# A reordered layer step, an earlier root chain, and six instead of five weight tiles in freed memory, in a two-layer hybrid backbone

## The chip, the cores and the metric

One core of a Trainium2 chip runs the whole program. The metric is the device time of one execution in microseconds, as the median of a few runs. The engines are TensorE (PE, matmuls, with PEld for its weight loads), VectorE (DVE), ScalarE (ACT), GpSimd (POOL) and SyncE (SP, which here only issues DMA). A second source of DMA is POOL, for gathers and scatters through an index.

## What is computed

Two layers over 512 latent tokens and 256 context tokens, 1024 wide. Each layer is a mixer and a mixture of experts (MoE):

```python
h  = rmsnorm(x) * modulation                      # latents and context apart
p  = h @ w_in                                     # split: q, k, v | z, xbc, dt
attn = diff_attend(rope(q), rope(k), v)           # 4 heads, each with its own rms norm
ssd  = gated_group_rmsnorm(mamba2_both_ways(conv(xbc), dt), z)
x += gate * (concat(attn, ssd) @ w_out)           # layer 1: the latents alone
h2 = rmsnorm(x) * modulation
aff = softmax(h2 @ w_router)                      # 16 experts
gate, idx = top_k(aff, 2 * n / 16)                # each expert takes 64 latent, 32 context rows
x[idx] += gate * ((silu(xe @ w_gate) * (xe @ w_up)) @ w_down)   # 1024 -> 1408 -> 1024
```

## The kernel before

All matmuls of the mixer are made of three in a short float format: an operand is split into a high part (`H`, `hi`, rounded by ACT) and a low part (`L`, `lo`, the rest, a subtraction on DVE or POOL), and `mm3` adds high x high, high x low and low x high. `Pieces` streams the mixer's weights: `fetch` issues the load of a piece (`raw`), `pull` rounds it on ACT (`rt<-raw`, L131), and the subtraction follows (L143), on POOL and DVE by turns.

The order of the work on each engine is the order in which the program issues it, moved by a scheduler with priorities (`tc.high_priority()`), and by hand in stretches under `manual_schedule`. Much of the program is generators: `q.tick(f, n)` takes n steps of a main stream `f` of matmuls and lets one step of each queued side job (`q.add(...)`) go between. A DMA that waits holds up every DMA behind it on SP. Pools of tiles (`pre`, `hp`, `op`, `rb`, `gx`) lie in one memory; a pool opened where another was released takes its addresses, and its first users wait for the last users of what lay there.

**The step between the layers.** Layer 0's MoE ends with the last expert's context rows: `yc` on PE (L1565), then the tail, `add_last` (L1688 on): a scaling on ACT, a multiplication by the gate vector on POOL (`rt<-rt`, L1692), and a scatter with addition into the context rows `xc` in DRAM (L1693). Layer 1 begins with `late_norm` (L837): four loads of latent rows (`xin`), their squares summed on ACT (L855) and DVE (L853, with a scratch tile `junk`), a chain of eleven tiny DVE instructions for the inverse root (`rsqrt_steps`, L204 to L223), the scaling of the rows (ACT L864, DVE L866), transposes (`trx`), then `H`, `h` and `L`, and the first projection (`xacc`). Two context tiles (`xin<-xc`) follow in the same way, once the scatter has landed.

**The heads' end.** Four heads (`hd[0]` to `hd[3]`) are projected and attended one after the other; `attend` stores its rows (`ob`) in DRAM (`mixd`). Then the output projection runs tile by tile: `op_in` loads a tile of 128 rows (`mixin<-mixd`), computes the roots of its group norms by the same chain (tags `mrs`), scales it on ACT (L1204), transposes it on PE (`mtr`, L1210) and splits it into `mT`; `op_tile` multiplies (`oacc`). `op_setup` beside it prepares the router: `wrA`, and `rbp` (L1172), sums over its columns for the latents and for the context.

**The MoE's weights.** Per expert there are eight pairs of gate and up tiles (`gw`, 1.44 MB a pair) and eleven w_down tiles (`rt`, `wd`, 0.52 MB each). The pairs rotate through nine buffers: `ngw` in pool `rb`, the rest in `gx`, one more elsewhere. `rb` takes the memory of the heads, which comes free while the output projection runs; `gx` that of the output weights, free only at its end. `cut` says in which ticks the pairs of expert 0 are asked for.

## Time and profile before

| | |
|---|---|
| median of 3 runs | 2394.22 us (2391.91 to 2396.35) |
| the profiled execution | 2389.74 us, span 2388.0 us |
| mean granted PE clock in it | 0.970 |
| busy share of the span | PE 91%, DVE 39%, ACT 27%, POOL 18% |
| bytes moved | 701.69 MB, 294 GB/s over the span |
| mixer of layer 0, MoE of layer 0 | 0 to 545 us, 545 to 1276 us |
| mixer of layer 1, MoE of layer 1 | 1276 to 1720 us, 1720 to 2388 us |

PE's 91% is a mean over stages of different kinds. In the MoE stages the share of the DMA engines tells whether the stream of weights sets the pace; in the mixers the waits of PE are read one by one, with the engine that ended each.

### The profile page before, as it was taken

The numbers are of one execution on the slowest core, as the hardware profiler recorded it, in microseconds if no ns is written. First come the engines' busy times: TensorE is split into PE (matmuls) and PEld (weight loads), VectorE is DVE, ScalarE is ACT, GpSimd is POOL, SyncE is SP. The second block draws the span as 40 slices with busy tenths as digits, with TensorE's granted clock in tenths as the row PEclk, the third lists the DMA queues.
The fourth block names the chain that finished last, engine by engine and source line by source line (L and its number), as shares of the span: only waits on it lengthen the run. The fifth ranks groups of instructions, "written<-read, shape, count | busy, mean of one in ns | idle before, by whom it ended". The sixth has DMA issues, their size and how long they took to land. (4 is left out here: it accounts for less than half of the span.)

```text
span 2388.0 us, 49731 instructions
## 1 busy us (share of the span) xinstructions
PE 2176.3 (91%) x20620; PEld 1247.0 (52%) x20620; DVE 931.7 (39%) x2586; ACT 652.2 (27%) x1791; POOL 433.5 (18%) x554
## 2 busy tenths in 40 slices
PE   6898998999999999999987988989799999988776
PEld 4677788685444444444435667877543333232322
DVE  5787578772111111111116786786611110101010
ACT  4434477532111111111113334575101010101000
POOL 4464342000101001001003464341000000000000
PEclk9999999999999999999998999999899999999999
DMA  7323723589999999999994226334999999999997
GB/s 250 91 78 102 266 72 107 186 285 344 390 407 401 398 405 393 401 400 400 395 390 127 86 66 198 112 109 139 347 400 416 385 416 410 416 411 415 412 413 314
DMA packets 229790, 701.69 MB, mean 294 GB/s; under 512 B 30340, under 2 KB 79324, under 8 KB 229564
## 3 DMA queue, kind: packets, MB, share of 16 engines
q1 hardware_dynamic: 220076, 681.37, 73.9%
q0 software_dynamic: 9488, 17.14, 3.5%
q8 instruction: 163, 2.67, 0.4%
q14 instruction: 63, 0.52, 0.1%
HBM read 674.66 MB, written 23.76 MB: 292 GB/s over the span
## 5 line engine op out<-in xcount | busy, mean ns | idle before, releaser
L1518 PE MATMUL gl<-gw,xeT 128*32 128x512 f32 (+1 forms) x8192 | 654.8, 466 | 61.9 <-DMA gw<-w_up 59.1
L1518 PEld LDWEIGHTS gl<-gw,xeT 128*32 128x32 f32 x8192 | 279.1, 111 | 441.4 <-issue 396.5
L1559 DVE SCALAR_TENSOR_TENSOR th<-th,gl 128x256 f32<-128x256 f32 (+1 forms) x96 | 37.5, 391 | 698.5 <-ACT th L1558 698.4
L1572 PE MATMUL yl<-rt,hl 128*32 128x512 f32 x2040 | 257.7, 595 | 9.5 <-PE gl L1518 9.2
L1558 ACT ACTIVATE th<-gl 128x256 f32<-128x256 f32 (+1 forms) x96 | 35.1, 366 | 768.1 <-PE gl L1518 761.4
L179 PE MATMUL pacc<-rt,H 128*128 128x384 f32 (+1 forms) x768 | 203.1, 346 | 7.1 <-POOL rt L143 2.4
L1699 DVE SCALAR_TENSOR_TENSOR ys<-yl,gate,G2l 128x512 f32<-128x512 f32 x32 | 24.0, 751 | 380.5 <-PE yl L1572 367.4
L1609 PE MATMUL gc<-gw,xeT 128*32 128x352 f32 x2048 | 171.2, 459 | 0.0
L1700 POOL DMA_INDIRECT out<-ys,sidx x16 | 24.8, 1549 | 730.6 <-DVE ys L1699 589.8
L179 PEld LDWEIGHTS pacc<-rt,H 128*128 128x128 f32 x768 | 134.1, 192 | 19.8 <-issue 6.0
L1572 PEld LDWEIGHTS yl<-rt,hl 128*32 128x32 f32 x2040 | 70.4, 109 | 141.3 <-issue 83.2
L179 PE MATMUL xacc<-H,rt 128*128 128x512 f32 (+1 forms) x448 | 135.9, 381 | 7.0 <-ACT H L816 6.6
L1456 POOL DMA_INDIRECT xe<-xn2d,gidx x16 | 15.1, 943 | 617.6 <-PE xet L1466 507.0
L179 PE MATMUL pacc<-rt,L 128*128 128x384 f32 (+1 forms) x384 | 127.1, 331 | 0.0
L1471 ACT ACTIVATE xeT<-xet,MC,A 128x64 f32<-128x64 f32 (+1 forms) x256 | 74.1, 426 | 178.5 <-PE xet L1466 178.5
L143 POOL TENSOR_TENSOR rt<-raw,rt 128x384 fp32r<-128x384 f32 (+1 forms) x88 | 101.5, 1176 | 80.7 <-ACT rt L131 66.4
L179 PE MATMUL oacc<-woh,mT 128*128 128x512 f32 x304 | 107.4, 411 | 0.0
L1572 PE MATMUL yl<-wd,hl 128*32 128x512 f32 x776 | 102.2, 599 | 2.2 <-DMA wd<-w_down 1.7
L1609 PEld LDWEIGHTS gc<-gw,xeT 128*32 128x32 f32 x2048 | 68.8, 110 | 56.6 <-issue 44.8
L179 PEld LDWEIGHTS xacc<-H,rt 128*128 128x128 f32 x448 | 83.1, 199 | 22.9 <-ACT H L816 7.4
L179 PE MATMUL xacc<-L,rt 128*128 128x512 f32 (+1 forms) x224 | 82.6, 371 | 3.0 <-POOL L L879 2.1
L1485 PE MATMUL xpk<-x,one 128*64 128x512 f32 x256 | 81.8, 633 | 3.4 <-DVE one L1481 3.4
(410 smaller groups left out, 3279.0 us busy)
## 6 DMA issues: line engine op xcount, KB each, us to landing
gw<-w_gate SPq DMA_DIRECT2D x256, 704.0 KB
gw<-w_up SPq DMA_DIRECT2D x256, 704.0 KB
rt<-w_down SPq DMA_DIRECT2D x255, 512.0 KB
wd<-w_down SPq DMA_DIRECT2D x97, 512.0 KB
mr<-w_mod SPq DMA_DIRECT2D x80, 512.0 KB
raw<-w_in SPq DMA_DIRECT2D x48, 256.0 KB
raw<-w_in SPq DMA_DIRECT2D x64, 192.0 KB
RB<-acsd SPq DMA_DIRECT2D x20, 512.0 KB
```

Of the source, the lines that this page charges most:

```text
L143: e.tensor_tensor(lo.bitcast(F32R), x, hi, op=OP.subtract)
L179: self.nc.tensor.matmul(o, a[x].bitcast(F32R), b[y].bitcast(F32R), start=start and i == 0, stop=stop and i == 2, **kw)
L1456: self.nc.gpsimd.indirect_dma_start(out=xe[0:n], out_offset=None, in_=self.xn2d[0:rows], in_offset=bass.IndirectOffsetOnAxis(ap=idx[0:n, e ...
L1471: nc.scalar.activation(xT[:, kk, c:d], tr[:, k, c - a:d - a], AF.Identity, scale=self.A2[:, s, kk:kk + 1], bias=self.MC[:, l, s, 24 + kk:2 ...
L1485: nc.tensor.matmul(ps[64 * j:64 * j + 64], one[:, t], self.x1[t][:, 512 * j:512 * j + 512], start=t == 0, stop=t == NL - 1, skip_group_che ...
L1518: self.nc.tensor.matmul(gl[c][32 * j:32 * j + 32, o:o + n].rearrange("p (u t i) -> p u t i", u=2, i=32), self.xT[:, k, 32 * g:32 * g + 32] ...
L1558: nc.scalar.activation(th, g, AF.Tanh, scale=0.5)
L1559: nc.vector.scalar_tensor_tensor(th, th, 1.0, g, op0=OP.add, op1=OP.mult)
L1572: nc.tensor.matmul(y[64 * j + 32 * g:64 * j + 32 * g + 32], h[:, g, b], wd[b][:, 512 * j:512 * j + 512], start=b == 0, stop=b == NF - 1, s ...
L1609: nc.tensor.matmul(gc[u][32 * j:32 * j + 32].rearrange("p (t i) -> p t i", i=32), xT[:, k, 64:96], w, start=k == 0, stop=k == KD - 1, skip ...
L1699: nc.vector.scalar_tensor_tensor(ys, y, self.gate[:, i, e:e + 1], G2[i], op0=OP.mult, op1=OP.mult)
L1700: nc.gpsimd.indirect_dma_start(out=dst[i], out_offset=bass.IndirectOffsetOnAxis(ap=self.sidx[:, i, e:e + 1], axis=0), in_=ys, in_offset=No ...
```

## The change

Three places are edited. At the **layer step** the two scratch tiles of the squares are allocated ahead of the x tiles; the last expert's tail runs inside `late_norm`, between the squares and the root chain, as one DVE instruction instead of one on ACT and one on POOL; the chain is issued in one piece ahead of the first weight subtractions; and the low parts of the first two weight pieces (`quiet`) are made on DVE. At the **heads' end** the roots of the first tile are computed by `mix_roots` in the last head's last tick (tags `mrt`), the store of `ob` is issued a step earlier, `op_setup` begins two steps earlier and leaves the context's half of `wrA` and `rbp` out in layer 1, where no context row is projected, and the first output tile takes its matmuls a little earlier. In the **MoE's weights** six pairs instead of five go to the heads' memory, and two instead of three to `gx`.

```diff
@@ Pieces.__init__ / pull
-        self.net, self.todo, self.raw, self.turn, self.low = net, iter(loads), [], 0, None
+        self.net, self.todo, self.raw, self.turn, self.low, self.quiet = net, iter(loads), [], 0, None, 0
...
-        pool = self.turn % 2 or x.shape[-1] == 384 if scale is None else scale is False
+        pool = (self.turn % 2 or x.shape[-1] == 384 if scale is None else scale is False) and self.turn > self.quiet
@@ run, start of layer 1
                 with tc.high_priority():
                     next(ln)
+                W.quiet = 2
                 ws = [xbc_weights(0)]
-                self.tail()
                 next(ln)
@@ run, heads
+        self.roots = {}
...
+                    if h == 3 and tk == 11:
+                        q.add(self.first_of(self.mix_roots(l, 0)))
                     q.tick(f, 4)
...
-        cut = [range(0, 2), range(2, 4), range(4, 5)] if l == 0 else [range(0, 5)]
+        cut = [range(0, 2), range(2, 4), range(4, 6)] if l == 0 else [range(0, 6)]
...
                 if i == 0:
-                    n = (2, 1)[j > 5] if j > 1 else 0
+                    n = (2, 1)[j > 3] if j > 0 else 0
@@ late_norm
+        junks = [pre.tile([P, D], BF16, name=f"junk{i}") for i in range(2)]
         xs = [pre.tile([P, D], F32, tag="xin", name="xin", bufs=NT) for _ in range(NT)]
...
-                junk = pre.tile([P, D], BF16, tag=f"junk{t % 2}", name="junk")
+                junk = junks[t % 2]
...
             if a == 0:
+                self.tail()
+            with self.tc.high_priority():
+                rs = self.rsqrt(pre, ss[:, a:a + n], n, 1.0 / D, f"rs{a}")
+            if a == 0:
                 yield
                 load(range(NL, NT))
             with self.tc.high_priority():
-                rs = self.rsqrt(pre, ss[:, a:a + n], n, 1.0 / D, f"rs{a}")
@@ op_setup
         yield
-        yield
-        yield
...
-        for s in range(2):
+        for s in range(1 if l else 2):
@@ new, and op_in
+    def mix_roots(self, l, t):
+        n = 6 if t >= NL else 5
+        self.roots[t] = yield from self.rsqrt_steps(self.lp, self.mss[:, t, 0:n], n, 1.0, "mrt")
...
-        rs = yield from self.rsqrt_steps(op, self.mss[:, t, 0:n + 2], n + 2, 1.0, f"mrs{n}")
-        yield
+        if t in self.roots:
+            rs = self.roots[t]
+        else:
+            rs = yield from self.rsqrt_steps(op, self.mss[:, t, 0:n + 2], n + 2, 1.0, f"mrs{n}")
+            yield
@@ add_last
-        nc.scalar.activation(ys, y, AF.Copy, scale=self.gate[:, 1, e:e + 1])
-        nc.gpsimd.tensor_tensor(ys, ys, g2, op=OP.mult)
+        nc.vector.scalar_tensor_tensor(ys, y, self.gate[:, 1, e:e + 1], g2, op0=OP.mult, op1=OP.mult)
...
-    ngw = 5
+    ngw = 6
@@ Head.attend, after ob and its square
+        if not own:
+            n.st(n.mixd[self.l][t * P:(t + 1) * P, P * self.h:P * self.h + P], ob)
         yield
...
-            return
-        n.st(n.mixd[self.l][t * P:(t + 1) * P, P * self.h:P * self.h + P], ob)
```

What the scheduler makes of it at the places that matter here. First the layer step on SP, the difference with each row's waits; `xin` are the latent rows, `raw` the first weight pieces. The names of the waits are counters: DMAHW and DMASW of DMA queues, the others of engines.

```order
 L162 DMA xin<-xr 128x1024 [waits DMASW4_49,DMASW5_49,DMASW3_49,DMASW6_49,DMASW2_49,DMASW7_49,DMASW1_49,DMAHW1_49,DMASW0_49,PE_49]
-L162 DMA xin<-xr 128x1024 [waits DMAHW2_49]
+L162 DMA xin<-xr 128x1024 [waits DMAHW2_49,DMAHW0_49,PE_49]
 L162 DMA xin<-xr 128x1024 [waits DMAHW3_49]
 L162 DMA xin<-xr 128x1024 [waits DMAHW4_49]
 L162 DMA raw<-w_in 128x4x128 [waits DMAHW5_49,DVE_49]
-L162 DMA raw<-w_in 128x4x128 [waits DMAHW6_49,PE_49,Activation_49]
+L162 DMA raw<-w_in 128x4x128 [waits DMAHW6_49,Activation_49]
 L162 DMA raw<-w_in 128x4x128 [waits DMAHW7_49]
```

The loads stand in the same order, but the second `xin` waits now for PE as well. The same place on DVE, before (from the squares L853 to the scaling L866, the chain's middle left out):

```order
L853 SCALAR_TENSOR_TENSOR junk,ss<-xin 128x1024 x2
L143 TENSOR_TENSOR rt<-raw,rt 128x512
L204 TENSOR_SCALAR rs_m<-ss 128x4
L206 TENSOR_SCALAR rs_y<-rs_m 128x4
...
L217 SCALAR_TENSOR_TENSOR rs_y<-rs_q,rs_y 128x4
L143 TENSOR_TENSOR rt<-raw,rt 128x512
L219 TENSOR_TENSOR rs_e<-rs_y 128x4
L221 TENSOR_TENSOR rs_e<-rs_e,rs_h 128x4
L223 SCALAR_TENSOR_TENSOR rs_y<-rs_e,rs_y 128x4
L866 TENSOR_SCALAR xin<-xin,rs_y 128x512 x4
```

and of the change (squares L857, scaling L873; L1704 is the tail):

```order
L857 SCALAR_TENSOR_TENSOR junk_12712,ss<-xin 128x1024 x2
L1704 SCALAR_TENSOR_TENSOR rt<-yc,gate_5699,rt 128x256
L204 TENSOR_SCALAR rs_m<-ss 128x4
L206 TENSOR_SCALAR rs_y<-rs_m 128x4
...
L219 TENSOR_TENSOR rs_e<-rs_y 128x4
L221 TENSOR_TENSOR rs_e<-rs_e,rs_h 128x4
L223 SCALAR_TENSOR_TENSOR rs_y<-rs_e,rs_y 128x4
L143 TENSOR_TENSOR rt<-raw,rt 128x512 x2
L873 TENSOR_SCALAR xin<-xin,rs_y 128x512 x4
```

The two weight subtractions (L143) have moved out of and ahead of the chain to behind it, and the tail stands ahead of the chain. Then DVE at the end of layer 1's heads, before; `KK` and `QL` are the last head's operands, `nm` the maximum that its exponentials need, `mrs` and `qrs` two root chains:

```order
L1808 TENSOR_TENSOR KK<-qtr,KK 64x256 x2
L1810 TENSOR_TENSOR QL<-qtr,Q 64x256 x2
L1832 TENSOR_REDUCE nm<-sc 128x2
L1759 TENSOR_REDUCE qss<-sq 128x4
L1833 SCALAR_TENSOR_TENSOR nm<-nm,rq 128x2
L204 TENSOR_SCALAR mrs_m<-mss 128x5
L204 TENSOR_SCALAR qrs_m<-qss 128x8
L145 SCALAR_TENSOR_TENSOR rt<-raw,wmix,woh 128x512
```

and of the change, where `mrt` is the first tile's root chain:

```order
L213 TENSOR_TENSOR mrt_e<-mrt_e,mrt_m 128x5
L215 SCALAR_TENSOR_TENSOR mrt_q<-mrt_e 128x5
L217 SCALAR_TENSOR_TENSOR mrt_y<-mrt_q,mrt_y 128x5
L219 TENSOR_TENSOR mrt_e<-mrt_y 128x5
L1820 TENSOR_TENSOR KK<-qtr,KK 64x256
L221 TENSOR_TENSOR mrt_e<-mrt_e,mrt_h 128x5
L1820 TENSOR_TENSOR KK<-qtr,KK 64x256
L223 SCALAR_TENSOR_TENSOR mrt_y<-mrt_e,mrt_y 128x5
L1822 TENSOR_TENSOR QL<-qtr,Q 64x256 x2
L1844 TENSOR_REDUCE nm<-sc 128x2
L1771 TENSOR_REDUCE qss<-sq 128x4
L1845 SCALAR_TENSOR_TENSOR nm<-nm,rq 128x2
```

The chain for the first tile stood behind the maximum and its products and shared DVE with `qrs`; it ends now ahead of `QL`. Last, SP at the entry of layer 0's MoE, before, `G2l` and `G2c` being gate vectors:

```order
L162 DMA gw<-w_up 128x1408
L162 DMA rt<-w_down 128x1024
L162 DMA xr<-ctx 128x1024
L169 DMA xc<-x_5933 128x1024
L162 DMA rt<-w_down 128x1024 x3
L162 DMA gw<-w_gate 128x1408
L162 DMA gw<-w_up 128x1408
L169 DMA xn2d<-xn 128x1024
L162 DMA gw<-w_gate 128x1408
...
L162 DMA G2c<-modd 32x256 x4
L162 DMA rt<-w_down 128x1024 x2
L162 DMA wd<-w_down 128x1024 x3
```

and of the change:

```order
L162 DMA gw<-w_gate 128x1408
L162 DMA xr<-ctx 128x1024
L162 DMA gw<-w_up 128x1408
L169 DMA xc<-x_5933 128x1024
L162 DMA rt<-w_down 128x1024
L162 DMA gw<-w_gate 128x1408
L162 DMA gw<-w_up 128x1408
L169 DMA xn2d<-xn 128x1024
L162 DMA gw<-w_gate 128x1408
...
L162 DMA G2c<-modd 32x256 x4
L162 DMA rt<-w_down 128x1024 x5
L162 DMA wd<-w_down 128x1024 x3
```

The sixth pair stands ahead of the first w_down tile (`rt`), and three more w_down tiles stand behind `G2c`.

## Rows read from the trace of the kernel before

**Rows 1.** The page: DMA engines' busy tenths in 40 equal slices.
```profile
DMA  7323723589999999999994226334999999999997
```

**Rows 2.** Windows: PE, PEld, DVE, ACT, POOL busy; clock, DMA share, GB/s.
```profile
540.00:544.00 4.00, 2.69 (x15) 2.58 (x16) 1.67 (x10) 0.31 (x2) 0.77 (x1) 0.50 0.27 80
1720.00:1724.00 4.00, 3.42 (x10) 1.38 (x12) 1.19 (x5) 0.00 (x0) 0.00 (x0) 0.50 1.02 413
1728.00:1732.00 4.00, 3.92 (x46) 2.10 (x50) 1.52 (x7) 2.50 (x9) 0.00 (x0) 1.00 0.15 59
```

**Rows 3.** PE's timeline, step: start, us, instruction, idle before and releaser.
```profile
1274.00 1.94 PE L1565 MATMUL yc<-wd,hc 128*32 128x256 f32 x32
1287.40 2.82 PE L872 MATMUL trx<-ident,xin 128*128 128x128 f32 x12 [11.47 <-ACT xin L864]
```

**Rows 4.** Timeline of PE at the heads' ends of both layers.
```profile
408.03 1.33 PE L1210 MATMUL mtr<-ident,mixin 128*128 128x128 f32 x5 [2.19 <-ACT mixin L1204]
...
1608.65 1.75 PE L1210 MATMUL mtr<-ident,mixin 128*128 128x128 f32 x7 [7.99 <-ACT mixin L1204]
...
1616.12 3.64 PE L1172 MATMUL rbp<-wr,MC 128*128 128x16 f32 x32
```

**Rows 5.** Timeline of SP's queue at the step.
```profile
1265.76 2.58 SPq L162 DMA_DIRECT2D xin<-xr  x4
1268.45 3.74 SPq L162 DMA_DIRECT2D raw<-w_in  x4
...
1285.21 0.80 SPq L162 DMA_DIRECT2D xin<-xc  x2
```

**Rows 6.** Timeline of ACT at the step, the latents' squares.
```profile
1270.10 1.06 ACT L855 ACTIVATE junk<-xin 128x1024 bf16<-128x1024 f32 x1 [1.02 <-DMA xin<-xr]
...
1273.20 1.06 ACT L855 ACTIVATE junk<-xin 128x1024 bf16<-128x1024 f32 x1 [1.95 <-DMA xin<-xr]
```

**Rows 7.** Timeline of DVE at the step, squares, chain and scaling.
```profile
1275.99 1.23 DVE L853 SCALAR_TENSOR_TENSOR junk<-xin 128x1024 bf16<-128x1024 f32 x1 [4.80 <-PE yc L1565]
...
1277.26 2.17 DVE L853 SCALAR_TENSOR_TENSOR junk<-xin 128x1024 bf16<-128x1024 f32 x1
...
1280.75 3.82 DVE L207 TENSOR_SCALAR rs_h<-rs_m 128x4 f32<-128x4 f32 x1
1284.48 0.16 DVE L209 TENSOR_SCALAR rs_y<-rs_y 128x4 int32<-128x4 int32 x1
...
1285.43 0.69 DVE L143 TENSOR_TENSOR rt<-raw,rt 128x512 fp32r<-128x512 f32 x1
...
1286.43 0.16 DVE L223 SCALAR_TENSOR_TENSOR rs_y<-rs_e,rs_y 128x4 f32<-128x4 f32 x1
1286.62 1.67 DVE L866 TENSOR_SCALAR xin<-xin,rs_y 128x512 f32<-128x512 f32 x4
```

**Rows 8.** Timeline of POOL at the step, scatter and weight subtracts.
```profile
1280.28 1.74 POOL L1693 DMA_INDIRECT xc<-rt,sidx  x1 [0.28 <-POOL rt L1692]
1281.46 3.06 POOL L143 TENSOR_TENSOR rt<-raw,rt 128x512 fp32r<-128x512 f32 x2
```

**Rows 9.** Groups of PE, 1286 to 1316 us: busy, mean ns | idle, releaser.
```profile
L179 PE MATMUL xacc<-L,rt 128*128 128x512 f32 (+1 forms) x32 | 11.6, 375 | 2.1 <-POOL L L879 2.1
```

**Rows 10.** Timeline of ACT at layer 1's heads' end and a later mixin.
```profile
1600.65 0.38 ACT L1864 ACTIVATE ob<-po,rr 128x128 f32<-128x128 f32 x1
...
1604.21 0.98 ACT L1837 ACTIVATE e<-sc,nm,rq 128x768 f32<-128x768 f32 x1
...
1608.09 1.79 ACT L1204 ACTIVATE mixin<-mixin,mrs_y 128x256 f32<-128x256 f32 x5 [2.55 <-DVE mrs_y L223]
...
1668.16 0.91 ACT L1204 ACTIVATE mixin<-mixin,mrs_y 128x256 f32<-128x256 f32 x2 [1.50 <-DMA mixin<-mixd]
```

**Rows 11.** Timeline of SP's queue, mixin loads of layer 1.
```profile
1598.54 0.90 SPq L162 DMA_DIRECT2D mixin<-mixd  x2
...
1665.51 0.80 SPq L162 DMA_DIRECT2D mixin<-mixd  x2
```

## The prediction

> **What bounds the kernel now.** I read the slices of the page first. The DMA line [rows 1] stands at 9 from the 10th to the 21st slice and again from the 29th to the last but one: those are the two MoE stages, in which 256 pairs of gate and up tiles stream in. The windows say how full that is: 1720 to 1724 us moves 413 GB/s at a share of 1.02 [rows 2]. Once such a stream runs without a gap, the end of its stage is the start of the stream plus bytes over rate. So an edit pays only if it lets the stream start earlier, or takes a gap out ahead of it. Gaps do stand there: 540 to 544 us has a share of 0.27 (2.9 us unused) and 1728 to 1732 us one of 0.15 (3.4 us unused) [rows 2]. In the second, all eight tiles are loaded and the next loads wait until the first expert's matmuls release one. The mixer sets that moment, so what the mixer saves ahead of it arrives at the end nearly whole.
>
> Next I looked where the mixers stand still. At the step between the layers TensorE (PE) ends the last expert's context rows (yc) at 1274.00 + 1.94 = 1275.94 and is idle for 11.47 us, until ScalarE (ACT) has scaled the first x tile [rows 3]. At the heads' end PE is idle 7.99 us in layer 1 and 2.19 us in layer 0 [rows 4], both times for the scaling of the mixin tile on ACT.
>
> **The step between layers.** The four x tiles are asked for from 1265.76, the first four weight pieces from 1268.45 [rows 5]. The first square starts at 1270.10 (4.34 us after the load's issue), the third tile's at 1273.20: one tile each 1.55 us [rows 6]. VectorE (DVE) begins its two squares at 1275.99 because its scratch tile lies where a w_down tile of the yc matmuls was, and ends them at 1277.26 + 2.17 = 1279.4. Then comes the root chain. Its steps take 0.16 us each at some 0.2 us spacing, but one lasts 3.82 us, from 1280.75 to 1284.57, while GpSimd (POOL) runs a scatter and two weight subtracts (1280.28 to 1284.52) [rows 7, 8]. The first scaling by the roots starts at 1286.62.
>
> The change takes the 0.69 us subtract out of the chain's middle [rows 7], and the last expert's tail off ACT and POOL. Had it done only this, the chain could end at about 1279.4 + 0.5 + 11 x 0.19 = 1282.0, and with two subtracts (0.65 each) ahead of the scaling, that would begin at 1283.3, 3.3 us earlier. But the scratch tiles now come first in the memory, so the x tiles lie further up, and the order of SP shows the price: the second x load now waits for PE as well. I take that for the last yc matmul, since the tile under it is the last w_down tile. So the second, third and fourth x load and the four weight pieces queued behind them leave SP not right after the first, at about 1266.5, but at 1276.0. Counted on with 4.34 and 1.55 us they are there at 1280.3, 1281.9 and 1283.4, and the last square (1.23 us alone) ends at 1284.6, 5.2 us later than now. The tail's one DVE instruction has no row: 128x256 lies between a step of 0.16 us and a square of 128x1024 at 1.23 [rows 7]; I take 0.45. Then the chain, 2.1, and the two subtracts, 1.3: scaling from 1288.5, **1.9 us later** than now, if POOL leaves the chain alone.
>
> It need not: the scatter (1.74 us) now starts when the chain does, and a weight subtract of POOL (1.53) follows [rows 8]. Bounds: nothing, or both, 3.3 us, as one step now loses 3.66. I take the middle, 1.6: scaling 3.5 us later. The Trainium skill (SBUF — State Buffer, "Who interferes with whom") says that a DVE instruction with two SBUF inputs, or in a two-port mode, and a GpSimd instruction that reads SBUF exclude each other, the later one waiting for the other's end. The step of 3.82 us agrees with it; by that rule the whole 3.3 us would be lost, and it is a reason to keep that bound. Nothing in the rows of the chain shows whether a scatter alone does this.
>
> PE gets part back. From 1287.40 it is busy but for 2.1 us in which it waits for the low halves (L) from POOL [rows 9], and DVE now makes all latent rows first, with the context's square (1.23) and chain (2.1) moved behind them. So 0 to 2.1 us returns; I take 1.0. The context itself starts some 2 us later, behind latent matmuls that have also moved: no cost. The xc loads (1285.21 now [rows 5]) wait for the scatter and move by over 4 us, covered by the same latent matmuls. Sum of the step: **+2.5 us** (1.9 - 2.1, so about 0, to 1.9 + 3.3 = 5.2).
>
> **The heads' tails.** The first tile's roots are now computed among the last head's work, so the scaling no longer waits for the chain (1608.09 in layer 1), but for ACT's turn. ACT has the exponentials until 1604.21 + 0.98 = 1605.2 [rows 10]. They come later now, since eleven DVE instructions (at most 11 x 0.19 = 2.1 us, at least nothing where DVE waited) stand ahead of the maximum that they need; I take 1.3. Scaling from 1606.5: 1.6 us gained in layer 1 (0 to 2.9). The mixin load must be there. It stood at 1598.54; now SP has the store of ob ahead of it, and ob is written at 1600.65 + 0.38. So it leaves at about 1601.5 and, with the 2.65 us that a later pair took (1665.51 to 1668.16), lands at 1604.2 [rows 10, 11]: 1.0 us before even the present end of the exponentials, which covers it. Layer 1 also drops half of the rbp matmuls, half of 3.64 us at 1616.12 [rows 4]; other PE work is at hand behind them, so I count 1.15 (0 to 1.8). Together **-2.75** (0 to -4.7). In layer 0 the same move can win at most the 2.19 us before mtr: **-1.5** (0 to -2.2). The refilled schedule of the first output tile costs no instruction; the cover is that the same matmuls run anyway, and at worst it gives nothing.
>
> **Six tiles in the heads' memory.** No byte is added. Of the weight tiles of expert 0 the sixth is loaded before most w_down tiles. In layer 0 three of them move behind G2, 3 x 0.524 MB at 413 GB/s = 3.8 us of stream; ahead of G2 the sixth tile (1.44 MB) fills their place. If SP still keeps the queue filled, 0; if the DMA runs dry between 544 and 554 us, +3.8; the 2.9 us at 540 us [rows 2] could at best be filled. I take **0**, since SP issues as fast as loads land there. In layer 1 two w_down tiles (2.5 us) move, and the 3.4 us unused at 1728 hide that: 0.
>
> **Sum:** 2.5 - 2.75 - 1.5 + 0 = -1.75 us on the profiled 2389.74, 2388.0. The median of the three runs is 4.5 us above that execution; on it the forecast is 2392.5, called **2392**: less than the 0.2% (4.8 us) that a measurement of this kernel can tell from no change.
>
> **Rivals.**
> (a) *The tails give all that they can* and the chain runs clear of POOL: step +1, tails -4.7 and -2.2, so -5.9: 2388. For it: PE is truly idle in both places. Against: ACT is busy until just before. Chance 0.22.
> (b) *The second x load does not bind*, because the matmul that it waits for is an earlier one. Then scaling starts 3.3 us earlier, as above, and PE gets the same 1.0 back behind it: -4.3, and with the tails -8.55: 2386. Against: the wait is in the order's row, and the matmul that I name is the last use of the tile under it. Chance 0.12.
> (c) *The chain sticks behind POOL*, the other side: all three squares late (1284.6), the tail 0.45, the scatter holds the chain for 1.74, one step again loses 3.66 to POOL's subtracts, then 2.1 and 1.3: scaling at 1293.8, 7.2 us late. The context's chain, behind the latent rows now, meets POOL's L subtracts in the same way and adds up to 3.3: +10.5 - 4.25 = +6.2: 2400. It decides if the first scaling comes after 1292.4 (5.8 late, which with 3.3 is past the tails' 4.25 plus 4.8). Against: SP's late loads also make POOL's subtracts late, so they may fall behind the chain. Chance 0.20.
> (d) *Nothing of it is seen*: the six tiles only reorder the stream, the tails' gain and the step's loss cancel. That is the forecast's own case, 0.46.
>
> **The numbers.** The forecast is 2392 (0.46). (a) and (b) make 0.34 faster, (c) 0.20 slower, 0.46 within. Its own range, from the bounds that partly cancel, is 2387 to 2397; with (a) and (b) at all their bounds together (-4.3 - 4.7 - 2.2 = -11.2: 2383, and the median of few runs adds 2 to 3 us either way) and (c) up to its time, 2380 to 2400: outside it is half of (c) and little of (b).
>
> **What the profile after would show.** The second x load issued at 1276, not 1266; the last square of the latents ending near 1284.6, scaling at 1288.5 to 1292, and PE idle for 13 to 16 us instead of 11.5. At the heads' end, the wait of 7.99 us split, mtr starting near 1607 in layer 1 and 406.5 in layer 0. No new DMA gap of over 1 us between 544 and 572. The forecast is wrong if x loads leave at 1266 (then b), if PE waits after the latent rows (c), or if the mixin tile lands after the exponentials, which would take the tails' gain away.

## The result and the profile after

The changed kernel takes 2406.71 us (median of 7 runs, 2401.37 to 2409.99), the kernel before 2391.96 (7 runs on the same chip): ratio 1.0064, interval 1.0054 to 1.0074, some 15 us slower. The forecast was 2392 within 2380 to 2400. It was wrong, and the time lies past the rival on the slow side (2400). The profiled execution has a span of 2407.5 us, 19.5 over that of before, so it is a long one of its seven; its parts are read below against two profiles of before. Against the first of these the 19.5 us lie at four places: 6.6 up to the first release of a weight tile in layer 0's MoE (574.89 before, 581.52 now), 4.6 at the step between the layers, 3.7 in the heads of layer 1, where nine profiles with these heads as before differ by 3.4 among themselves, and 5.8 at the heads' end. The rest of layer 0's MoE took 1.5 less, and behind the first router matmul of layer 1 it is 0.3.

The page's DMA line (for [rows 1]), and behind it the windows at layer 0's MoE entry (columns as in [rows 2]):

```profile
DMA  7223722679999999999994226333899999999997
```

The windows:

```profile
540.00:544.00 4.00, 2.19 (x20) 2.08 (x20) 2.87 (x13) 0.96 (x3) 0.97 (x1) 0.96 0.78 262
544.00:548.00 4.00, 0.53 (x5) 0.53 (x6) 2.64 (x16) 0.31 (x2) 0.00 (x0) 0.50 1.02 330
...
576.00:580.00 4.00, 4.00 (x61) 2.54 (x57) 0.72 (x2) 0.69 (x2) 0.00 (x0) 1.00 0.48 140
580.00:584.00 4.00, 4.00 (x63) 1.92 (x59) 2.48 (x9) 0.41 (x2) 0.00 (x0) 1.00 0.36 107
```

The gap of [rows 2], in which the first gather runs, is filled, as the change has it: share 1.02 from 544 to 548. But PE is busy for only 0.53 of these four us (2.69 in the gap before), and a new gap of 4.6 us has opened at 576 to 584. What was put into the first gap came out of the second; e4, with the six tiles alone, has its second gap at 572 to 580 (shares 0.64 and 0.32).

The step between the layers, PE's timeline (for [rows 3]; `dtr`, the first transposes of the time steps, is a landmark 36 us further on):

```profile
1279.10 1.94 PE L1578 MATMUL yc<-wd,hc 128*32 128x256 f32 x32
1293.39 0.69 PE L879 MATMUL trx<-ident,xin 128*128 128x128 f32 x2 [12.35 <-ACT xin L871]
...
1333.24 0.44 PE L918 MATMUL dtr<-ident,dtq 128*128 128x128 f32 x2
```

SP's queue at the same place (for [rows 5 to 8], as the next three):

```profile
1270.96 11.40 SPq L162 DMA_DIRECT2D xin<-xr  x4
1282.46 2.35 SPq L162 DMA_DIRECT2D raw<-w_in  x4
```

ACT there, the scaling:

```profile
1292.61 2.56 ACT L871 ACTIVATE xin<-xin,rs_y 128x512 f32<-128x512 f32 x4 [2.14 <-DVE rs_y L223]
```

DVE there, the last square, the tail, the chain's first step and its long one:

```profile
1287.58 1.23 DVE L857 SCALAR_TENSOR_TENSOR junk<-xin 128x1024 bf16<-128x1024 f32 x1 [1.68 <-DMA xin<-xr]
...
1288.73 0.48 DVE L1704 SCALAR_TENSOR_TENSOR rt<-yc,gate,rt 128x256 f32<-128x256 f32 x1
1289.12 0.16 DVE L204 TENSOR_SCALAR rs_m<-ss 128x4 f32<-128x4 f32 x1
...
1290.71 1.67 DVE L221 TENSOR_TENSOR rs_e<-rs_e,rs_h 128x4 f32<-128x4 f32 x1
```

POOL there:

```profile
1289.49 1.57 POOL L1705 DMA_INDIRECT xc<-rt,sidx  x1 [20.81 <-DVE rs_y L206]
1290.56 1.79 POOL L143 TENSOR_TENSOR rt<-raw,rt 128x512 fp32r<-128x512 f32 x1
```

The four x loads take 11.40 us to leave, and the weight pieces leave behind them at 1282.46, after the end of yc (1281.04), where before they had gone 7.5 us ahead of it. The last square ends 7.8 us after yc, the chain keeps its 0.2 us spacing beside the scatter, and loses 1.5 us in one step beside POOL's subtraction. ACT scales at once behind the chain.

Layer 1's heads' end, first PE's timeline (for [rows 4]; the views of ACT, SP and DVE further on are for [rows 10, 11]):

```profile
1612.66 1.50 PE L1872 MATMUL po<-V,wT 128*128 128x128 f32 x12
...
1622.13 1.76 PE L1223 MATMUL mtr<-ident,mixin 128*128 128x128 f32 x7 [7.97 <-ACT mixin L1217]
1623.68 1.06 PE L1867 MATMUL wtr<-ident,e 128*128 128x128 f32 x4
...
1626.82 3.43 PE L1177 MATMUL rbp<-wr,MC 128*128 128x16 f32 x16
...
1632.79 2.76 PE L1872 MATMUL po<-V,wT 128*128 128x128 f32 x12
```

The same matmuls before, beside `mtr` in [rows 4]; `wtr` transposes the attention's weights, which `po` then multiplies:

```profile
1598.14 1.50 PE L1860 MATMUL po<-V,wT 128*128 128x128 f32 x12
1599.47 0.60 PE L1855 MATMUL wtr<-ident,e 128*128 128x128 f32 x4
...
1610.20 2.77 PE L1860 MATMUL po<-V,wT 128*128 128x128 f32 x12
```

Windows behind `mtr`, two of the changed kernel and one of before (columns as in [rows 2]):

```profile
1622.13:1626.13 4.00, 2.84 (x12) 2.16 (x13) 3.93 (x22) 2.91 (x7) 0.76 (x2) 0.50 0.88 294
1630.13:1634.13 4.00, 4.00 (x15) 3.52 (x16) 1.85 (x7) 0.00 (x0) 0.56 (x1) 0.50 0.33 110
1612.65:1616.65 4.00, 4.00 (x26) 3.50 (x25) 3.86 (x9) 3.23 (x9) 2.00 (x2) 0.87 0.65 203
```

ACT there:

```profile
1619.62 0.99 ACT L1849 ACTIVATE e<-sc,nm,rq 128x768 f32<-128x768 f32 x1 [2.36 <-DVE nm L1845]
...
1621.58 1.78 ACT L1217 ACTIVATE mixin<-mixin,mrt_y 128x256 f32<-128x256 f32 x5
```

SP's queue there:

```profile
1616.86 0.33 SPq L169 DMA_DIRECT2D mixd<-ob  x1
1617.23 1.06 SPq L162 DMA_DIRECT2D mixin<-mixd  x2
```

DVE there, two steps of the first tile's chain and what stands behind it:

```profile
1613.10 1.20 DVE L215 SCALAR_TENSOR_TENSOR mrt_q<-mrt_e 128x5 f32<-128x5 f32 x1
...
1615.82 0.17 DVE L223 SCALAR_TENSOR_TENSOR mrt_y<-mrt_e,mrt_y 128x5 f32<-128x5 f32 x1
1616.00 0.88 DVE L1822 TENSOR_TENSOR QL<-qtr,Q 64x256 fp32r<-64x256 f32 x2
1616.91 1.76 DVE L1844 TENSOR_REDUCE nm<-sc 128x2 f32<-128x1536 f32 x1
```

PE still waits 7.97 us (7.99 before), though the scaling no longer waits for roots. The roots are ready at 1615.99, but `QL` and the maximum stood behind their chain, so the exponentials are late, and ACT scales only after them. Counted from the last `po` ahead of the wait, `mtr` does come 1.0 us sooner (9.47 us behind its start, 10.51 before). But `wtr`, which ran inside the wait before, stands behind `mtr` now, and the next `po`, which followed `mtr` after 1.55 us, follows after 10.66. Half of the rbp matmuls is gone, and the other half takes nearly as long as all did (3.43 us, 3.64 before): it stands now where the granted clock is at 0.50, the lower of PE's two levels (1.2 GHz; 1.00 is 2.4). Behind `mtr` the clock is back at 1.00 after some 5 us before; in the changed kernel, where PE waits once more between `mtr` and rbp, it stays at 0.50 for over 12.

### The profile page after: what moved, and what is told of

The parts are those of the page before. It is cut to its first block, busy times and chain, and to the rows that moved or that the text cites. A ratio compares the mean times of both kernels' runs of the same rounds, so it can differ in the third digit from the quotient of the medians.

```text
span 2407.5 us, 49671 instructions
## 1 busy us (share of the span) xinstructions
PE 2185.1 (91%) x20604; PEld 1254.2 (52%) x20604; DVE 929.1 (39%) x2586; ACT 653.7 (27%) x1790; POOL 430.1 (18%) x552
## 4 chain that ended last, share of the span: by engine, by line
PE 47%; DMA 32%; DVE 11%; issue 4%; ACT 3%; POOL 2%; SPq 0%; POOLq 0%; DVEq 0%; ACTq 0%
PE gl L1531 12%; DMA gw<-w_up 10%; DMA gw<-w_gate 9%; DMA rt<-w_down 7%; PE yl L1585 6%; PE pacc L179 5%; PE oacc L179 4%; PE gc L1622 4%; DMA wd<-w_down 3%; PE yc L1578 2%; PE xpk L1498 2%; PE xacc L179 2%; PE po L1872 2%; PE sc L1840 2%; PE macc L335 1%
## 5 line engine op out<-in xcount | busy, mean ns | idle before, releaser
L1531 PE MATMUL gl<-gw,xeT 128*32 128x512 f32 (+1 forms) x8192 | 655.2, 466 | 59.0 <-DMA gw<-w_up 57.3
L1469 POOL DMA_INDIRECT xe<-xn2d,gidx x16 | 15.1, 945 | 618.5 <-PE xet L1479 508.8
L143 POOL TENSOR_TENSOR rt<-raw,rt 128x384 fp32r<-128x384 f32 (+1 forms) x87 | 99.8, 1162 | 66.1 <-ACT rt L131 64.7
```

The costliest lines, as they stand in the source:

```text
L143: e.tensor_tensor(lo.bitcast(F32R), x, hi, op=OP.subtract)
L1531: self.nc.tensor.matmul(gl[c][32 * j:32 * j + 32, o:o + n].rearrange("p (u t i) -> p u t i", u=2, i=32), self.xT[:, k, 32 * g:32 * g + 32] ...
```

## The experiments

**The parts.** First each of the three parts alone: e1 the layer step, e3 the heads' end, e4 the six tiles; e2 is e1 with one line moved:

```diff
-        junks = [pre.tile([P, D], BF16, name=f"junk{i}") for i in range(2)]
         xs = [pre.tile([P, D], F32, tag="xin", name="xin", bufs=NT) for _ in range(NT)]
+        junks = [pre.tile([P, D], BF16, name=f"junk{i}") for i in range(2)]
```

*e1, the hunks of late_norm, add_last, Pieces and the start of layer 1.* 

> The kernel before with the layer step of the change alone. Theory A (the loss sits in the step: x loads held by the last yc matmul, and the context's norm behind the latents on DVE): +7 to +10 us, as the two traces show between the end of yc and the middle of layer 1's mixer. Rival B (the step costs what the forecast said, and the loss lies in the heads' tails and the weight tiles): +1 to +4 us.

*e2, e1 with the x tiles ahead of the scratch tiles.* 

> The same step, with the x tiles allocated ahead of the scratch tiles again, so that no x load waits for PE. Theory A1 (the held load is the cause): the x loads leave at about 1266 us again, and the step ends 0 to 5 us faster than before. Rival A2 (the order on DVE is the cause, with the context's square, chain and scaling behind all latent rows): the first scaling comes 3 us earlier than before, but the context comes late all the same, and the time is +2 to +6 us.

*e3, the hunks of mix_roots, op_in, op_setup, attend and the fill.* 

> The kernel before with the heads' end of the change alone. Theory C (the tails lose, because attention work that ran in the idle time now stands behind the scaling, and the first tile's matmuls are spent early): +4 to +8 us, over both layers. Rival (the forecast): -4 us.

*e4, `ngw` and `cut`.* 

> The kernel before with six weight tiles in the heads' memory alone. Theory D (three w_down tiles behind the gate vectors let the DMA run dry at layer 0's MoE entry): +2 to +4 us. Rival (the forecast, hidden): within 1.5 us of before.

A ratio given here is not the quotient of the two medians and can lie up to 0.001 from it (e7, e10), so a difference of 2 us isn't to be read from one ratio. Measured against 2390.79 us: e1 1.0018 (1.0009 to 1.0028), e2 0.9992 (0.9982 to 1.0001), e3 1.0020 (1.0008 to 1.0032), e4 1.0025 (1.0015 to 1.0035). That is +4.3, -1.9, +4.8 and +6.0 us. e1, e3 and e4 together make 15.1, the change 15.3: within their intervals the parts add, and each of the three is a loss. e1 came out between its theory (7 to 10) and its rival, e4 above both of its cases, and by another mechanism than its theory's: the DMA didn't run dry at the entry (shares of 0.97 to 1.00 from 540 to 552). One line's place, the order of two allocations, is worth 6 us (3 to 9 by the two intervals): with the x tiles first, SP's loads leave ahead of yc again (SP's timeline of e2), and PE waits 7.53 us, not 13.57 as in e1.

```profile
1265.24 2.50 SPq L162 DMA_DIRECT2D xin<-xr  x4
1267.85 5.09 SPq L162 DMA_DIRECT2D raw<-w_in  x4
```

**The step's other half.** e9 is e2 with the low parts of the first pieces on POOL and DVE by turns, as before:

```diff
-                W.quiet = 2
+                W.quiet = 0
```

> The step alone with the x tiles ahead of the scratch tiles, as in the earlier kernel of that kind (0.9992, -1.9 us), and with the low parts of the first weight pieces on POOL and DVE by turns as before the change (quiet at 0). The order of DVE shows what else moves: the context's square and chain stand among the latent rows' h and L again, no longer behind them. Theory A2: the part of the step that was costed at nothing, the late context, takes back what the chain gains. In the earlier kernel the first transpose of the x tiles came 4.0 us sooner after the yc matmuls than before the change, and the context's projection about as late as before. Then this kernel keeps the context early: the context's first projection comes 3 to 4 us sooner after yc than before the change, and the time is 4 to 6 us under before (0.9975 to 0.9983). Rival A3 (the forecast's rival c): a POOL subtraction beside the chain holds one of its steps for 1.5 to 3.7 us, so the first scaling comes 2 to 4 us later than in the earlier kernel, and the time is that of before or over (0.9995 to 1.0015).

Measured 0.9994 (0.9985 to 1.0003), against e2's 0.9992: the same time by both ways, and both theories half right. DVE's chain in e9, its two long steps:

```profile
1277.63 1.20 DVE L206 TENSOR_SCALAR rs_y<-rs_m 128x4 int32<-128x4 int32 x1
...
1279.46 2.41 DVE L215 SCALAR_TENSOR_TENSOR rs_q<-rs_e 128x4 f32<-128x4 f32 x1
```

POOL in e9 at the same time:

```profile
1277.54 1.26 POOL L143 TENSOR_TENSOR rt<-raw,rt 128x512 fp32r<-128x512 f32 x1 [16.32 <-ACT rt L131]
1278.97 1.57 POOL L1696 DMA_INDIRECT xc<-rt,sidx  x1 [0.17 <-DVE rs_h L207]
1280.01 1.84 POOL L143 TENSOR_TENSOR rt<-raw,rt 128x512 fp32r<-128x512 f32 x1
```

And in e2, where POOL has one subtraction, this and the long step of DVE's chain:

```profile
1279.69 1.85 POOL L143 TENSOR_TENSOR rt<-raw,rt 128x512 fp32r<-128x512 f32 x1
```

```profile
1279.51 2.06 DVE L217 SCALAR_TENSOR_TENSOR rs_y<-rs_q,rs_y 128x4 f32<-128x4 f32 x1
```

Each POOL subtraction holds one step of the chain to its own end (1278.80 and 1278.83; 1281.85 and 1281.87 in e9, 1281.54 and 1281.57 in e2), the scatter none. So the first transposes come 8.9 us after yc in e9 and 7.5 in e2 (11.5 before). But from these to `dtr` it is 36.1 us before, 39.2 in e1 and e2, 39.9 in the changed kernel and 36.9 in e9: with `quiet` the context's square and chain come last on DVE, and PE is slower behind the first transposes. What `quiet` gains ahead of the first transpose, 1.4 us, it loses behind it, 2.3; the times can't tell the two apart.

**The heads' end, edit by edit.** e5 is e3 without the refilled schedule, e6 the early roots alone:

```diff
-                    n = (2, 1)[j > 3] if j > 0 else 0
+                    n = (2, 1)[j > 5] if j > 1 else 0
```

> The heads' end of the change, but the first output tile keeps its old schedule of matmuls (none in the first two ticks, two at a time until the sixth). Theory C1 (the new schedule spends the first tile's matmuls before the late attention comes, and PE stands still behind them): the loss of 5 us falls to between -2 and +1.5. Rival C2 (it is the root chain ahead of the last head's maximum, which makes the exponentials and with them the scaling late): the loss stays at +3 to +6.

> The early root chain alone: mix_roots and its use in op_in; the store, the setup's two steps, the halved rbp and the schedule of matmuls are as before. Theory C2 (the chain delays the exponentials): +1 to +4 us. Theory C1: within 1.5 us of before, or 1 to 3 us faster, as the forecast had it.

Measured 1.0021 (1.0008 to 1.0035) and 0.9999 (0.9988 to 1.0011): neither the fill nor the roots by themselves are what loses by these times, and the roots win nothing. Then e10 is e3 without the earlier start of `op_setup`, e11 e3 with the store of `ob` where it was:

```diff
@@ e10, op_setup
         yield
+        yield
+        yield
@@ e11, Head.attend
-        if not own:
-            n.st(n.mixd[self.l][t * P:(t + 1) * P, P * self.h:P * self.h + P], ob)
         yield
...
+            return
+        n.st(n.mixd[self.l][t * P:(t + 1) * P, P * self.h:P * self.h + P], ob)
```

> The heads' end alone, all of it but the earlier start of op_setup (its two steps stay). The part alone with the earlier start was 1.0020 (+4.8 us), the roots alone 0.9999. Theory C3: the loss is the early router setup: rbp and wrA come between the first mixin tile's transposes and the late attention, at the low clock, and push the first output tile back. Then this kernel is at or under the time before: 0.9985 to 1.0002 (half of the rbp matmuls gone, 1.8 to 3.4 us, the rest as before), and the stretch from the first mixin transpose of layer 1 to the first router matmul is 53 to 55 us, as before, not 59. Rival C4: the early store, which stands on SP ahead of the mixin load, is what loses: then it stays at 1.0015 to 1.0025 and the stretch at 58 to 60.

> The heads' end alone, all of it but the earlier store of ob, which stays where it was, a step later than the attention's output. Theory C3 (the early setup loses): 1.0015 to 1.0025, as the whole part (1.0020), and 58 to 60 us from the first mixin transpose of layer 1 to its first router matmul. Rival C4 (the store ahead of the mixin load loses): 0.9985 to 1.0005, the mixin loads of layer 1 leaving SP about 1 us sooner and the stretch at 53 to 55 us.

Measured 0.9999 (0.9991 to 1.0008) and 1.0009 (1.0000 to 1.0018): taking the setup back brings the time to that of before (by the medians it stays 2.2 us over); what the store's place is worth beside the others, 2.6 us by the ratios, isn't clear of noise. The stretch from the first mixin transpose to the first router matmul, which both theories named, stayed long in both, 57.4 and 55.6 us (59.5 in e3), so it doesn't separate them: the roots lengthen it already (57.3 in e6 alone). The last three take single edits: e13 only the halved rbp (`range(1 if l else 2)`), e14 this and the two `yield`s gone, e15 the early store alone.

> One edit alone: the context's half of wrA and rbp is left out in layer 1. Theory C5: it brings more than its matmuls. In the step's kernel with it, the 16 that stay took 1.85 us (32 took 3.64 before), 1.8 less, and the granted clock, which fell to 0.60 in the four us behind the 32, stayed at 1.00; the stretch from the first mixin transpose to the first router matmul of layer 1 was 49.9 us, not 53.0 to 53.3. So 3.1 us under before: 0.9984 to 0.9990, and no stretch under 0.9 of the clock between 1616 and 1626. Rival: only the matmuls count, 1.8 us: 0.9991 to 0.9995.

> The halved rbp and the earlier start of op_setup, nothing else. Theory C3: the earlier start loses by itself, since rbp and wrA then stand right behind the first mixin transposes, where the clock is still at 0.50: the 16 rbp matmuls take 3.4 us in place of 1.85, DVE's two wrA products come ahead of the mixin's split, and attention's po comes later. So 3 to 5 us over the kernel with the halved rbp alone, that is 1.0000 to 1.0008 of before. Rival: the setup loses only beside the early roots, then it equals the halved rbp alone within 0.0005.

> The earlier store of ob alone. On SP it stands between the two halves of the mixin load of layer 1 then, where the second half waits until ACT has written ob. Theory C4 in its small form: it loses 1 to 3 us, 1.0004 to 1.0012, by loads that leave SP late (the second mixin half near 1601.5, not 1599; the four raw pieces of w_out behind it too). Rival: nothing is late that is waited for, 0.9996 to 1.0003.

Measured 0.9987 (0.9978 to 0.9996), 0.9984 (0.9975 to 0.9993), 1.0008 (0.9998 to 1.0018). The store's 1.9 us aren't sure, since its interval holds 1; its mixin load does leave late, at 1603.32, but the scaling comes 9.95 us behind the last `po` as before. The halved rbp brings 3.1 us; its interval would allow the rival's 1.8 too, but the stretch of the profile, 49.9 us where six kernels with the heads' end of before have 52.9 to 53.5, says 3.0 to 3.6 as well. PE's rows in e13, rbp and the next `po`:

```profile
1615.72 1.85 PE L1172 MATMUL rbp<-wr,MC 128*128 128x16 f32 x16
...
1618.66 1.50 PE L1860 MATMUL po<-V,wT 128*128 128x128 f32 x12
```

The window behind it in e13:

```profile
1620.20:1624.20 4.00, 4.00 (x29) 2.75 (x31) 2.49 (x3) 1.73 (x5) 2.11 (x2) 1.00 0.56 162
```

And the same window in e8, a second profile of the kernel before, with the same `po` in the first profile:

```profile
1619.90:1623.90 4.00, 4.00 (x20) 3.74 (x19) 2.44 (x5) 0.67 (x3) 2.40 (x3) 0.59 0.14 55
```

```profile
1621.12 2.76 PE L1860 MATMUL po<-V,wT 128*128 128x128 f32 x12
```

1.8 us is the matmuls' own (3.64 for all in [rows 4]); behind all 32 the granted clock is 0.59 over four us, behind 16 it stays at 1.00. The remaining 1.3 us are in the `po` behind, 1.50 us where it took 2.76. The early setup beside the halved rbp loses nothing by the times: my theory of it fell. PE in e14:

```profile
1610.97 3.56 PE L1170 MATMUL rbp<-wr,MC 128*128 128x16 f32 x16 [6.55 <-DMA wr<-w_router]
...
1614.80 1.73 PE L1208 MATMUL mtr<-ident,mixin 128*128 128x128 f32 x7
```

Here rbp runs slowly too, but ahead of `mtr`, for the most part inside the wait (`mtr` comes 2.2 us later behind the last `po` than in e13). With the early roots, `mtr` comes first and rbp stands behind it, between it and all that the heads' late attention needs. Worked out from the ratios: roots 0, halved rbp -3.1, setup -0.7 to 0, store +1.9, the fill -0.2 (e3 against e5), which makes -1.4 to -2.1; measured are +4.8. So some 6 us seem to come only from edits together, but each term has an interval of 2 to 4 us either way. e10 against e3 puts 5.0 (1.5 to 8.5) on the setup beside all the others; no run has it beside the roots alone.

The traces hold a finer measure: from the start of the last `po` ahead of the wait to the first router matmul of layer 1. Seven profiles with the heads' end of before take 63.6 to 64.0 us, and from that router matmul to the end of the span all 17 profiles take 726.2 to 728.3, so in a profile what is lost in the stretch arrives at the end.

| edits at the heads' end | stretch, us |
|---|---|
| none (seven profiles) | 63.6 to 64.0 |
| the halved rbp (e13, e12) | 60.7, 60.5 |
| the store (e15) | 63.6 |
| the halved rbp and the setup (e14) | 62.2 |
| the roots (e6) | 66.8 |
| all but the setup (e10) | 66.8 |
| all but the store (e11) | 65.0 |
| all but the fill (e5) | 68.3 |
| all (e3, the changed kernel) | 68.9, 68.3 |

By this measure the whole loses 4.2 to 5.4 us, as by the time, but the roots alone lose 3, and beside them the gain of the halved rbp is gone. The times of e6 and e10 don't show these 3 us (by the medians 0.0 and 2.2; the profiled run of e6 is the slowest of its ten). So it is shown that the edits lose together, and in which stretch; how the loss divides among roots, setup and store stays open.

**The six tiles, and the best of it.** e7 has six tiles in layer 1 only; e12 is e2 with the halved rbp:

```diff
@@ e7, run
+        self.ngw = 5 + l
-        cut = [range(0, 2), range(2, 4), range(4, 5)] if l == 0 else [range(0, 5)]
+        cut = [range(0, 2), range(2, 4), range(4, 5)] if l == 0 else [range(0, 6)]
```

> Six weight tiles in the heads' memory in layer 1 alone, five in layer 0. Theory D1 (the loss is layer 0's: the sixth tile's successors fill the DMA engines while the first gathers of routed rows run, and PE waits for the gathers 2 us longer each): within 1.5 us of before. Rival D2 (both layers lose): +2 to +4 us.

> The kernel before, unchanged, for a second profile. Where the two profiles of the same kernel differ, a difference of the changed kernel's profile of that size explains nothing: in layer 1's mixer, from the last transposes of its norm to the heads' end, I expect 1 to 4 us of it.

> A version meant to be better than both: the step with the x tiles ahead of the scratch tiles, and of the heads' end the one edit that only takes work away, the context's half of wrA and rbp in layer 1 (16 of 32 matmuls, 3.64 us before for all, and one DVE product). Five tiles in the heads' memory, roots, store and setup as before. If the parts add as the three parts of the change did (4.3, 4.8 and 6 for 15.3 measured), it is the -1.9 us of the step and the -1.2 to -1.8 us of the matmuls: 0.9985 to 0.9988. Rival: the rbp matmuls fill time in which PE has nothing else, and nothing is added to the step's -1.9: 0.9990 to 0.9994.

e7 measured 1.0010 (0.9996 to 1.0024), its two medians 2390.26 and 2390.34. The ratio's 2.4 us lie in the rival's range, so the time doesn't decide. The traces do: with six tiles in layer 1 the stretch from its first router matmul to the end takes 727.1 us (e7, e4) and 726.6 (the changed kernel), with five 726.2 to 728.3; the stretch ahead of it, from the first `mtr`, is that of before (53.4). So by the profiles the loss of e4 is layer 0's. e8, the kernel before once more, took 2389.19 us; between `dtr` and `mtr` its profile is 1.8 us longer than the first one, as expected. e12 measured 0.9979 (0.9970 to 0.9988), the lowest ratio here: the sum of e2 (-1.9) and e13 (-3.1). By the medians, 2387.80 against 2390.72, it is 2.9 us. Either way it beats both kernels.

Where layer 0 loses shows on PE and SP in e4 (`xet` transposes the rows that POOL gathers for expert 0, of the latents and then of the context; the `gw` row is the first load into a tile that expert 0 has released):

```profile
543.39 1.11 PE L1466 MATMUL xet<-ident,xe 64*128 64x64 f32 x8 [3.35 <-DMA xe<-xn2d,gidx]
...
566.97 0.65 PE L1466 MATMUL xet<-ident,xe 32*128 32x32 f32 x8 [1.66 <-DMA xe<-xn2d,gidc]
```

```profile
577.78 0.33 SPq L162 DMA_DIRECT2D gw<-w_gate  x1
```

The first gather on POOL, in e4 and before:

```profile
538.21 0.97 POOL L1456 DMA_INDIRECT xe<-xn2d,gidx  x1 [109.94 <-DVE rs_y L223]
```

```profile
539.80 0.97 POOL L1456 DMA_INDIRECT xe<-xn2d,gidx  x1 [110.62 <-DVE rs_y L223]
```

And before, its `xet` on PE and the first load into a released tile on SP:

```profile
543.57 1.11 PE L1466 MATMUL xet<-ident,xe 64*128 64x64 f32 x8 [1.31 <-DMA xe<-xn2d,gidx]
```

```profile
574.89 0.33 SPq L162 DMA_DIRECT2D gw<-w_gate  x1
```

Before, this load left at 574.89, in e8 at 573.96, in the changed kernel at 581.52. And in all 17 profiles of this study the last yc matmul of layer 0 ends 698.8 to 701.2 us after it. So this one moment dates the whole stage. Counted from the last `po` ahead of layer 0's first `mtr`, the load leaves 181.4 us later in e4 and 183.0 in the changed kernel; with five tiles it is 176.8 to 179.0 in 14 of 15 profiles, and 180.7 in e14, whose early setup acts in layer 0 too. The gather took 3.8 us from issue to `xet` before (539.80 to 543.57), when the share was 0.27; 5.2 in e4 (from 538.21) beside a share of 0.97, 5.3 in the changed kernel. In the 15 profiles with five tiles in layer 0 it took 3.8 to 4.0. The Trainium skill (DMA: Bandwidth & Descriptors, "SWDGE vs HWDGE vs iDMA") has it that software and hardware queues are served in turn within each DMA engine; a gather that is slower beside a full stream agrees. The longer gather accounts for 1.4 us of the late release at most; the rest is open: e4's clock also fell to 0.57 from 568 to 572, behind the second wait, and e7, whose layer 0 is that of before, had waits of 2.69 and 1.24 with its release at 574.69.

## Why the prediction was wrong, by its steps

**The first views were read rightly; what they mean for layer 0 was not.** "The mixer sets that moment" was said of layer 1 alone. In layer 0 the stream was taken as bytes over rate, the 0.27 as room that "could at best be filled", and the six tiles at 0 (to +3.8). The failed step: in that room the gather ran, on which expert 0 hangs, and so the first release, and so the end. Measured: +6.0 us (e4), past the bound, of which the profile shows 2.9 to 3.8 at the release; at most 1.4 of these are the gather's, and the cause of the others stays open.

**Loads and squares.** The second x load waits for the last yc matmul, as read from the order: shown, and worth 6 us by e2. The last square came 7.8 us after yc (8.7 forecast), the tail took 0.48 (0.45). Rival (b) fell.

**The chain beside POOL.** The scatter holds nothing and one subtraction holds one step for 1.5 us: 1.6 in the sum was right, though by luck, for it was the middle between nothing and both, and rival (c), which had the scatter hold the chain as well, is not how the loss came. The Trainium skill's rule (SBUF — State Buffer, "Who interferes with whom") agrees for the subtractions, to 0.03 us at their ends, in e9 and e2. Its order, the later one waiting, doesn't show in the records: in e2, and for the second subtraction of e9, DVE's record begins 0.2 and 0.6 us ahead of POOL's.

**The scaling.** It came 11.6 us after yc, not 14.2: ACT doesn't stand behind DVE's two subtractions, which were counted on the path with 1.3. PE's wait at the first transpose grew by 0.9 us (2.1 in e1), not 3.5.

**"0 to 2.1 us returns; I take 1.0", the late context "no cost".** This is the step's failed term, in sign: between the first transpose and `dtr` PE loses 3.1 us in e1 and 3.8 in the changed kernel. Its waits for `L` didn't vanish, the group of [rows 9] read again:

```profile
L179 PE MATMUL xacc<-L,rt 128*128 128x512 f32 (+1 forms) x24 | 9.5, 418 | 3.3 <-POOL L L886 2.7 <-DVE L L886 0.5
```

The longest of them, 2.15 us at 1308.25, is for a latent `L` that stands behind two weight subtractions on POOL, and the granted clock is 0.86 and 0.72 in the eight us from 1305.39 (1.00 at that place before). The context's transposes begin without a wait. All waits of 0.15 us and more behind the first transpose make 2.5 us before, 3.6 in e1 and 4.1 in the changed kernel; the rest of the loss isn't traced. The step as forecast was +2.5, measured +4.3 (its upper bound was 5.2).

**The tails.** "Exponentials 1.3 later, 0 to 2.1" was right within its bound: counted from the last `po` they are 1.9 later in e6, for the chain's eleven steps don't stand at 0.19 each on an engine that does other work between (one took 1.20), and `QL` waits for all of them. "Scaling 1.6 us gained" had the right sign too: 1.0 in e6. The mixin load left after the store, as said, and didn't bind the scaling. The failed step is that a sooner scaling was booked as time gained, without asking what then stands behind `mtr`: `wtr`, done inside the wait before, and in the changed kernel rbp, all at a clock of 0.50, so that the next `po` comes 4.2 us behind `mtr` in e6 and 10.7 in the changed kernel instead of 1.55. The early roots are worth nothing by the time and cost 3 us by the profile (e6). The halved rbp was sized 1.15 and is 3.1 alone (e13), because of the clock behind it; in the change its 16 matmuls take 3.43 us behind `mtr`, and the gain is lost. "Together -2.75" and "-1.5" became +4.8. In layer 0 `mtr` comes 0.8 us sooner behind the last `po` (9.79, 10.61 before), but PE waits 7.27 us there in one piece, where it waited 4.68 and 2.19, and the first gather leaves 143.7 us behind that `po` (142.4): nothing gained. Not seen at all was that edits which are free or better alone lose 5 us together.

**The rivals** had the sign of neither tail nor tiles: no case put a loss there. The price of (c), 2400, was reached and passed by three small losses, which the forecast had as one gain (the tails), one zero (the tiles) and one small loss (the step). The range ended where one mishap ended.

## What to carry to other kernels

Before a DMA gap is filled, look for what runs in it: a gather on which the first release hangs is worth more than the bytes. When scratch is allocated ahead of load targets, look up whose last use now lies under each target, since one held load holds all behind it on its queue. A chain moved ahead on an engine that works in order delays what then stands behind it, and a matmul that comes sooner may push others behind itself into a stretch of low clock. So measure the whole stretch up to a fixed landmark and not the one wait, count from a landmark of the same profile since two profiles are shifted by some us, and test edits together, since those that are free alone may not be free together.

## What the runs showed of the hardware that was not expected

A DVE step of 0.16 us beside a POOL subtraction ended within 0.03 us of that subtraction's end, in e2, e9 and the changed kernel (1292.38 and 1292.35), also where its own record begins 0.2 to 0.6 us ahead of POOL's; beside a scatter of 1.57 us, none was held. Thirty-two matmuls of 16 columns on a PE that was busy throughout were followed by a granted clock of 0.59 over the next four us (mostly the lower of its levels of 1.2 and 2.4 GHz), sixteen by 1.00. A gather of 64 rows took 3.8 to 4.0 us from issue to its first user in 15 profiles, in which the DMA engines' share was at most 0.60 over its first four us, and 5.2 and 5.3 in the two where it was 1.02 and 1.03.
